# Turned results read two or three units later, and the last quarter of a merged sum turned on TensorE

## The chip, the cores and the metric

The kernel runs on one core of a Trainium2 chip. The metric is the device time of one execution in microseconds (us); the median of several runs is compared.

## The reference

Two decoder layers over 256 tokens of 2048 features, all in float32. Every layer normalises its input, projects it once to some 18,000 columns, and runs three token mixers on slices of that projection; each mixer's output is gated, projected to 2048 columns, weighted with a sigmoid gate and summed; a last projection is added to the input.

```
h = rms_norm(x, norm_w)
proj = h @ w_in
(qa, ka, va, za, qi, ki, wi, ub, zb, qc, kc, vc, zc, gates) = jnp.split(proj, split_points(), axis=-1)
qa = apply_rope(qa...); ka = apply_rope(ka...); qi = apply_rope(qi...); ki = apply_rope(ki...)
y_a = (dsa_attention(qa, ka, va, qi, ki, wi, top_k) * jax.nn.silu(za)) @ w_a_out
y_b = (conformer_conv(ub, conv_w, conv_b, cln_w, cln_b) * jax.nn.silu(zb)) @ w_b_out
y_c = (stick_breaking_attention(qc, kc, vc) * jax.nn.silu(zc)) @ w_c_out
g = jax.nn.sigmoid(gates).reshape(b, s, N_BRANCH, D_MODEL)
merged = g[:, :, 0] * y_a + g[:, :, 1] * y_b + g[:, :, 2] * y_c
return x + merged @ w_out
```

After the second layer comes a final RMSNorm. Branch A picks 64 keys per query with an indexer (qi, ki, wi); branch B is a causal depthwise convolution with 31 taps; branch C is stick-breaking attention.

## The kernel before, in words

**Weights.** Each projection is worked in *units*: 128x1024 weights are loaded into `raw` (four buffers, issued on SyncE), cast on ScalarE to the high part `wh` (`high`, L219), and VectorE takes the difference as the low part `wl` (`low`, L223), three buffers each. A unit's twelve matmuls (L233, in `token_products` or `chunk_T`) give the three products high x high, low x high and high x low. Eight units make a *chunk* of 512 columns. There are 733 units; TensorE runs them one after the other, and VectorE and ScalarE prepare the parts up to three units ahead.

**Turned results.** `chunk_N` leaves tokens on the partitions; most users want features there. `turned` (L255) does that off TensorE: two 32x32-block transposes on VectorE into `zt` (L266), four strided DMAs from GpSimd's queue into `z` in DRAM (L269), one fetch into `zy` (L271; `zt` and `zy` have one buffer each). What is done with `zy` is a generator, the *use*: rope for the queries of attention A (`rope_F`, L365), scaling or copying for C (L785, L834), the SiLU gate (`gate`, L402), a sigmoid and the product into `yT` for the convolution's input (L671, L674), the split of the merged sum (`use_m`, L938) and of the next layer's input (`x_parts_F`, L442).

**When a use runs.** `turned` first finishes any older use (`settle`), issues all five DMAs at once, and puts the use on the list `pending`, due `LATER` = 6 units on (10 for the convolution's input, 5 for the last quarter of the merged sum). After each unit, `background` takes the first use that is due, places its next step behind that unit's last matmul, and the step is scheduled with high priority. All queues are in order: an instruction that waits holds up everything behind it on its engine, weight parts too. A scheduler fixes the order at build time. A step ends at a `yield n`, and the next is due n units on.

**Other work behind the units.** `stages` holds generators for the attention, the indexer (`index_first`, `index`, with `choose`: eight rounds of MAX8 and MATCH_REPLACE8 on VectorE) and the convolution's norm; `waiting` holds the convolution's taps (L417, L419), of which one or two go behind each low part.

**The merged sum.** For each of four quarters `mg` holds the sum; the last branch in the order is B. When its quarter is added (L974, L975), `turned` and `use_m` make its parts `mx`. The output projection `w_out` begins right after the fourth quarter; its units need quarters 0 to 3 in turn, the seventh unit the first rows of quarter 3.

The functions that the diff touches and what calls them, with the line numbers of the profile:

Of the kernel before, what the change touches and what calls it, by code (L numbers as in the profile page):

```python
# [14 lines left out]
P = 128  # L15
# [9 lines left out]
TOPK = 64  # L25
TAPS = 31
PRE = 2
LATER = 6
EV, EV2 = (3,), (5,)
URGENT = 10 ** 6  # L30
PAD = TAPS - 1
# [18 lines left out]
def trunk(ctx: ExitStack, tc: tile.TileContext, x, w_in, xt, w_a, w_b, w_c, w_out,  # L50
# [38 lines left out]
    def nm(s):  # L89
        uid[0] += 1  # L90
        return f"{s}_{uid[0]}"
# [17 lines left out]
    def hi(b, k, n=1, ts=slice(0, S)):  # L109
        return part(b, 0, k, n, ts)  # L110

    def lo(b, k, n=1, ts=slice(0, S)):
        return part(b, 1, k, n, ts)
# [29 lines left out]
    pending = []  # L143

    def step_on(e):
        with tc.high_priority():
            try:
                e[0] = count[0] + next(e[1])
            except StopIteration:
                pending.remove(e)  # L150

    def settle():
        while pending:
            step_on(pending[0])

    def background(mm):
        for e in pending[:1]:
            if e[0] <= count[0]:
                with tc.issue_after(mm.ins):
                    step_on(e)  # L160
        for e in stages[:2]:
            if e[1] <= count[0]:
                with tc.issue_after(mm.ins):
                    advance(e)
                break
# [24 lines left out]
                f()  # L190

    newest = [None]

    def load_unit(w, k0, kn, segs, dst=None):
        n = sum(c for _, c in segs)
# [20 lines left out]

    def high(u):
        with tc.high_priority():
            nc.scalar.copy(u[1], u[0])  # L219

    def low(u):
        with tc.high_priority():
            sub = nc.vector.tensor_sub(u[2], u[0], u[1].bitcast(F32))  # L223
        drain(sub)

    def unit(*args, **kw):
# [27 lines left out]

    def turned(srcs, use, later=LATER):  # L255

        settle()
        n = len(srcs)  # L260
        tmp = tp.tile([P, n, 4, 4, 32], F32, tag="zt", bufs=1, name=nm("zt"))
        z = dp.tile([n, 4, 32, 4, P], F32, tag="z", bufs=4, name=nm("z"))
        y = tp.tile([P, n * 4, 4, 32], F32, tag="zy", bufs=1, name=nm("zy"))
        with tc.high_priority():
            for t, src in enumerate(srcs):
                nc.vector.transpose(tmp[:, t].rearrange("p b k i -> p k b i"),  # L266
                                    src.rearrange("p (k b c) -> p k b c", b=4, c=32))
            for a in range(4):
                nc.gpsimd.dma_start(z[:, :, :, a, :].rearrange("t b c e -> c (t b) e"),  # L269
                                    tmp[a * 32:(a + 1) * 32].rearrange("c t b k i -> c (t b) (k i)"))  # L270
            nc.gpsimd.dma_start(y.rearrange("p (t a) k i -> p t (a k i)", t=n),  # L271
                                z.rearrange("t b c a e -> (b c) t (a e)"))

        pending.append([count[0] + later, use(y)])

    def by_feature(y):
        return y.rearrange("p u k i -> p k u i")

    def blocks(v):
        return v.rearrange("p k (u i) -> p k u i", i=32)  # L280

    def chunk_F(w, c0, act, nk, use, later=LATER):
        turned(chunk_N(w, [(c0, 512)], act, nk), use, later)
# [74 lines left out]
    def split(h, l, src):  # L358
        nc.scalar.copy(h, src)  # L359
        nc.vector.tensor_sub(l, src, h.bitcast(F32))  # L360
# [4 lines left out]
    def rope_F(dst, y):  # L365
        s = t4().rearrange("p (u k i) -> p u k i", k=4, i=32)
        nc.scalar.copy(s[0:64], y[64:128])
        nc.scalar.copy(s[64:128], y[0:64])
        c, d = (v.rearrange("p (u i) -> p u i", i=32).unsqueeze(2).to_broadcast([P, S // 32, 4, 32])
                for v in (cos1, sin1))  # L370
        nc.vector.tensor_mul(y, y, c)
        yield 1
        nc.vector.tensor_mul(s, s, d)
        nc.vector.tensor_add(blocks(dst), by_feature(y), by_feature(s))

# [21 lines left out]
    def sigmoid_of(y):  # L397
        sg = t4().rearrange("p (u k i) -> p u k i", k=4, i=32)
        nc.scalar.activation(sg, y, AF.Sigmoid)  # L399
        return sg  # L400

    def gate(c0, o, b, w, hx):  # L402
        def use(k, y):
            sg = sigmoid_of(y)
            nc.vector.tensor_mul(y, y, sg)  # L405
            yield 1
            nc.vector.tensor_mul(y, y, blocks(o[:, k:k + 4, :]).rearrange("p k u i -> p u k i"))
            split(blocks(hi(b, k, 4)), blocks(lo(b, k, 4)), by_feature(y))

        for k in range(0, KC, 4):  # L410
            chunk_F(w, c0 + k * P, hx, KD, partial(use, k))

    def tap(yT, cv, pr, c, q):
        wq = pr[:, P_CW + c * TAPS + q:P_CW + c * TAPS + q + 1]
# [27 lines left out]
    def x_parts_F(xn, k, nw, y):  # L442
        xT, ux = xn
        xs = xT[k // KC][:, k % KC:k % KC + 4, :]
        nc.vector.tensor_mul(blocks(xs), by_feature(y), nw[:, k:k + 4].unsqueeze(2).unsqueeze(3).to_broadcast([P, 4, S // 32, 32]))
        split_at(ux, k, 4, xs)
        yield 1

    def ssq_total(ssq):
        s = small(2)[:, :ssq.shape[1]]  # L450
# [16 lines left out]
    for layer in range(DEPTH):  # L467
# [200 lines left out]

        def use_g(y):
            sg_u.append(sigmoid_of(y))  # L670
            yield 1  # L671

        def use_a(y, yT=yT):
            nc.vector.tensor_mul(blocks(yT[:, 4:8, PAD:]), by_feature(y), by_feature(sg_u.pop()))  # L674
            taps(1)
            yield 1

        sg_u = []
        with tc.high_priority():
# [1 line left out]
                nc.vector.tensor_mul(yT[:, i * 2:i * 2 + 2, PAD:], ua[i], sgs[i].rearrange("p (h t) -> p h t", h=2))  # L681
        taps(0)
        chunk_F(w, O_UG + 4 * P, hx, KD, use_g)
        chunk_F(w, O_UA + 4 * P, hx, KD, use_a, 10)


        qi = [slot(F32R).rearrange("p a b -> p (a b)").rearrange("p (h t) -> p h t", t=P) for _ in range(2)]
# [90 lines left out]

        qaT = slot()
        for h in range(0, NH, 4):  # L780
            chunk_F(w, O_QA + h * P, hx, KD, partial(rope_F, qaT[:, h:h + 4, :]))
        qcT = slot()

        def use_q(h, y, qcT=qcT):
            nc.scalar.mul(blocks(qcT[:, h:h + 4, :]), by_feature(y), SCALE)  # L785
            yield 1

        for h in range(0, NH, 4):
            chunk_F(w, O_QC + h * P, hx, KD, partial(use_q, h))
# [42 lines left out]

        def use_k(h, y, kcT=kcT):
            nc.scalar.copy(blocks(kcT[:, h:h + 4, :]), by_feature(y))  # L834
            yield 1

        for h in range(0, NH, 4):
            chunk_F(w, O_KC + h * P, hx, KD, partial(use_k, h))
# [98 lines left out]

        def use_m(j, y):  # L938
            split(blocks(hi(mx, j * 4, 4)), blocks(lo(mx, j * 4, 4)), by_feature(y))
            yield 1  # L940

        for b in (0, 2, 1):
            if b == 2:
                finish()
                settle()
                gc = parts(KC)
                gate(O_ZC, qcT, gc, w, hx)
            if b == 1:
                finish()
                settle()  # L950
                gb = parts(KC)
                gate(O_ZB, cv, gb, w, hx)
                mx = parts(KD)
            gx = ga if b == 0 else gc if b == 2 else gb
            for j in range(4):
                if b == 2 and j == 1:
                    finish()
                    flush()
                    start(conv_norm())
                g = chunk_N(w, [(O_G + b * D + j * 512, 512)], hx, KD)  # L960
                sg = [ev() for _ in range(NT)]
                with tc.high_priority():
                    for t in range(NT):
                        nc.scalar.activation(sg[t], g[t], AF.Sigmoid)  # L964
                if j == 0:
                    settle()
                y = chunk_N((w_a, w_b, w_c)[b][layer], [(j * 512, 512)], gx, KC)
                with tc.high_priority():
                    for t in range(NT):
                        dst = mg[j // 2][:, j % 2, t, :]  # L970
                        if b == 0:
                            nc.vector.tensor_mul(dst, y[t], sg[t])
                        else:
                            nc.vector.tensor_mul(sg[t], y[t], sg[t])  # L974
                            nc.vector.tensor_add(dst, dst, sg[t])  # L975
                if b == 1:
                    turned([mg[j // 2][:, j % 2, t, :] for t in range(NT)], partial(use_m, j), LATER if j < 3 else 5)


        last = layer == DEPTH - 1  # L980
# [21 lines left out]
        def emit_x(xc, accs, q, c0, ts):  # L1002
            n = xc.shape[-1]
            with tc.high_priority(offset=URGENT):
                for a_, t in zip(accs, ts):
                    nc.vector.tensor_add(xc[:, t, :], a_, xc[:, t, :])  # L1006
            if last:
                sq = ev()
                for t in ts:
                    with tc.high_priority(offset=URGENT):  # L1010
                        nc.scalar.activation(sq[:, :n], xc[:, t, :], AF.Square, accum_out=ssq[:, t, q:q + 1])
                    nc.vector.tensor_mul(xfr[t][:, c0:c0 + n], xc[:, t, :], fwr[:, c0:c0 + n])
            else:
                x_squares([xc[:, t, :] for t in ts], ssq, q, ts)
                if q < 3:
                    turned([xc[:, t, :] for t in ts], partial(x_parts_F, xn, c0 // P, nwn))

        def store_x(xc, c0):
            if not last:
# [98 lines left out]
```

## Time and profile before

| | us |
|---|---|
| median of 3 runs | 2071.09 |
| lowest, highest | 2069.34, 2073.09 |
| the profiled execution | 2067.06 |
| its span | 2065.1 |
| TensorE busy | 2039.8 |
| VectorE busy | 1498.5 |
| ScalarE busy | 1036.4 |

The span runs from the first to the last recorded instruction; 1.96 us lie around it. Busy time counts an engine's instructions, not its waiting; of TensorE's matmuls the ends are modelled, so that their starts are the better measure. In the profile PE is TensorE, PEld its weight load, DVE is VectorE, ACT is ScalarE, POOL is GpSimd, SP is SyncE, and L233 is line 233 of the kernel.

### The profile page before, as it was taken

Reading aid. Unit: us, or ns where it says so; the run is one execution under the profiler, and the core shown is the slowest. Engines: PE = TensorE matmul, PEld = TensorE weight load, DVE = VectorE, ACT = ScalarE, POOL = GpSimd, SP = SyncE. Lnnn points to the kernel's source line nnn. Section 1 sums busy time; section 2 is a strip of 40 time slices with the busy share of each in tenths; the row PEclk is TensorE's granted clock in tenths of the full one; section 3 lists DMA queues with packets and bytes.
Section 4 is the critical chain, followed back from the end, with each engine's and each line's share of the span. In section 5 each row is a group of like instructions: output and inputs, shape, how many; then the busy total and the mean of one; then the engine's idle time right before and its main releaser. Section 6 shows DMA issues by size and latency. Waiting matters only on the chain.

```text
span 2065.1 us, 26913 instructions
## 1 busy us (share of the span) xinstructions
PE 2039.8 (99%) x10064; PEld 1739.5 (84%) x10064; DVE 1498.5 (73%) x2026; ACT 1036.4 (50%) x1217; POOL 119.2 (6%) x199
## 2 busy tenths in 40 slices
PE   9999999999999999999999999999999999999998
PEld 9899878888888888888898998788888888888877
DVE  8768988688777855665676799886887678556555
ACT  7455445466444544444454654454664445444443
POOL 0100011010000001011101001110100000011000
PEclk9999999999999999999999999999999999999999
DMA  7777576665567567876767775766755665677764
GB/s 255 229 224 215 163 225 214 200 221 168 174 197 230 190 198 227 262 233 227 252 198 232 215 207 169 229 213 194 223 165 176 208 219 192 193 234 248 251 210 147
DMA packets 246531, 435.08 MB, mean 211 GB/s; under 512 B 19712, under 2 KB 69888, under 8 KB 246272
## 3 DMA queue, kind: packets, MB, share of 16 engines
q1 hardware_dynamic: 231632, 389.32, 59.3%
q0 software_dynamic: 13104, 40.91, 6.5%
q10 hardware_dynamic: 1664, 3.15, 0.4%
q8 instruction: 78, 1.28, 0.3%
q14 instruction: 53, 0.43, 0.1%
HBM read 408.67 MB, written 24.64 MB: 210 GB/s over the span
## 4 chain that ended last, share of the span: by engine, by line
PE 46%; DMA 2%; DVE 2%; issue 1%; ACT 0%; POOL 0%; DVEq 0%; POOLq 0%; ACTq 0%
PE acc L233 44%; DMA zy<-z 1%; DMA z<-zt 1%; DVE wl L223 1%; PE mm L764 0%; PE mm L797 0%; POOL z L269 0%; PE mm L822 0%; DVE zt L266 0%; PE mm L891 0%; PE mm L855 0%; DVE s L419 0%; DVE t L1006 0%; PE mm L814 0%; ACT wh L219 0%
## 5 line engine op out<-in xcount | busy, mean ns | idle before, releaser
L233 PE MATMUL acc<-wh,s 128*128 128x512 f32 (+2 forms) x4992 | 1222.4, 387 | 7.8 <-ACT wh L219 5.2
L223 DVE TENSOR_TENSOR wl<-raw,wh 128x1024 fp32r<-128x1024 f32 (+2 forms) x729 | 876.9, 1207 | 409.3 <-ACT wh L219 407.5
L219 ACT CAST wh<-raw 128x1024 fp32r<-128x1024 f32 (+2 forms) x728 | 756.3, 1043 | 796.8 <-PE acc L233 559.9
L233 PEld LDWEIGHTS acc<-wh,s 128*128 128x128 f32 x4992 | 923.5, 188 | 196.1 <-ACT wh L219 7.7
L233 PE MATMUL acc<-wl,s 128*128 128x512 f32 (+2 forms) x2496 | 658.1, 386 | 1.2 <-DVE wl L223 1.2
L233 PEld LDWEIGHTS acc<-wl,s 128*128 128x128 f32 x2496 | 464.2, 188 | 96.5 <-DVE wl L223 2.1
L419 DVE SCALAR_TENSOR_TENSOR s<-yT,cst,s 128x256 f32<-128x256 f32 x480 | 216.3, 478 | 0.4
L233 PE MATMUL acc<-s,wh 128*128 128x256 f32 (+2 forms) x1120 | 194.2, 320 | 0.0
L269 POOL DMA_DIRECT2D z<-zt x156 | 91.0, 590 | 1667.5 <-DVE zt L266 1520.2
L233 PEld LDWEIGHTS acc<-s,wh 128*128 128x128 f32 x1120 | 169.2, 191 | 3.4
L233 PE MATMUL acc<-s,wl 128*128 128x192 f32 (+1 forms) x864 | 115.9, 276 | 5.6 <-DVE wl L223 5.6
L233 PEld LDWEIGHTS acc<-s,wl 128*128 128x128 f32 x864 | 111.7, 191 | 8.5 <-DVE wl L223 7.6
L266 DVE STREAM_TRANSPOSE zt<-acc 128x512 f32<-128x512 f32 x56 | 39.8, 710 | 11.4 <-PE acc L233 11.4
L271 POOL DMA_DIRECT2D zy<-z x39 | 28.0, 719 | 193.7 <-DMA z<-zt 151.2
L359 ACT CAST s<-zy 128x1024 fp32r<-128x1024 f32 x20 | 21.0, 1050 | 32.1 <-DMA zy<-z 18.1
L360 DVE TENSOR_TENSOR s<-zy,s 128x1024 fp32r<-128x1024 f32 x20 | 24.5, 1223 | 16.7 <-ACT s L359 16.7
L974 DVE TENSOR_TENSOR ev<-acc,ev 128x512 f32<-128x512 f32 x32 | 22.0, 688 | 19.2 <-PE acc L233 19.2
L405 DVE TENSOR_TENSOR zy<-zy,t 128x1024 f32<-128x1024 f32 x12 | 14.7, 1224 | 18.9 <-ACT t L399 18.8
L399 ACT ACTIVATE t<-zy 128x1024 f32<-128x1024 f32 x14 | 14.9, 1061 | 26.5 <-DMA zy<-z 26.4
L964 ACT ACTIVATE ev<-acc 128x512 f32<-128x512 f32 x48 | 26.3, 591 | 0.0
L384 DVE TENSOR_TENSOR ev<-ev,cst 128x384 f32<-128x384 f32 (+2 forms) x20 | 11.2, 558 | 19.4 <-ACT ev L382 19.3
L975 DVE TENSOR_TENSOR s<-s,ev 128x512 f32<-128x512 f32 x32 | 21.9, 684 | 0.0
(203 smaller groups left out, 813.3 us busy)
## 6 DMA issues: line engine op xcount, KB each, us to landing
raw<-in_w_in_dram SPq DMA_DIRECT2D x555, 512.0 KB, 3.6
raw<-in_w_out_dram SPq DMA_DIRECT2D x64, 512.0 KB, 4.9
z<-zt POOLq DMA_DIRECT2D x156, 128.0 KB, 4.4
zy<-z POOLq DMA_DIRECT2D x39, 512.0 KB, 5.0
raw<-in_w_a_dram SPq DMA_DIRECT2D x32, 512.0 KB, 3.5
raw<-in_w_c_dram SPq DMA_DIRECT2D x32, 512.0 KB, 3.6
raw<-in_w_b_dram SPq DMA_DIRECT2D x32, 512.0 KB, 5.0
raw<-in_w_in_dram SPq DMA_DIRECT2D x16, 256.0 KB, 2.8
```

Of the source, the lines that this page charges most:

```text
L219: nc.scalar.copy(u[1], u[0])
L223: sub = nc.vector.tensor_sub(u[2], u[0], u[1].bitcast(F32))
L233: newest[0] = nc.tensor.matmul(o, lhsT, rhs, start=start, stop=stop, skip_group_check=True)
L266: nc.vector.transpose(tmp[:, t].rearrange("p b k i -> p k b i"), src.rearrange("p (k b c) -> p k b c", b=4, c=32))
L269: nc.gpsimd.dma_start(z[:, :, :, a, :].rearrange("t b c e -> c (t b) e"), tmp[a * 32:(a + 1) * 32].rearrange("c t b k i -> c (t b) (k i)"))
L271: nc.gpsimd.dma_start(y.rearrange("p (t a) k i -> p t (a k i)", t=n), z.rearrange("t b c a e -> (b c) t (a e)"))
L359: nc.scalar.copy(h, src)
L360: nc.vector.tensor_sub(l, src, h.bitcast(F32))
L419: nc.vector.scalar_tensor_tensor(o, yT[:, c, q:q + S], wq, o, op0=ALU.mult, op1=ALU.add)
L964: nc.scalar.activation(sg[t], g[t], AF.Sigmoid)
L974: nc.vector.tensor_mul(sg[t], y[t], sg[t])
L975: nc.vector.tensor_add(dst, dst, sg[t])
```

## The change

- A use, or the next step of one, is placed behind the newest unit's two parts (the copy of `high` and the difference of `low`) in the order, and no longer behind the newest unit's last matmul. All uses that are due go, not one per unit.
- `LATER` becomes 9. Gates, rope and the next layer's input use 8, the convolution's input 11. The single steps after a use (`yield 1` at its end) become `yield 0`, and in `rope_F` and `gate` the `yield 1` moves one operation up.
- `turned` no longer calls `settle`. The buffer `zy` is taken, and its fetch issued, in a first step two units after the transposes; the use is due later by the rest.
- The fourth quarter of the merged sum is no longer turned through DRAM: a stage `turn` transposes it in eight 128x128 pieces on TensorE, behind the second unit of the output projection, into PSUM, and splits it from there.

```diff
-LATER = 6
+LATER = 9
...
     def step_on(e):
-        with tc.high_priority():
+
+        with tc.high_priority(), tc.issue_after(newest_parts[0].ins), tc.issue_after(newest_parts[1].ins):
...
     def background(mm):
-        for e in pending[:1]:
-            if e[0] <= count[0]:
-                with tc.issue_after(mm.ins):
-                    step_on(e)
+        while pending and pending[0][0] <= count[0]:
+            step_on(pending[0])
...
-            nc.scalar.copy(u[1], u[0])
+            newest_parts[0] = nc.scalar.copy(u[1], u[0])
...
-            sub = nc.vector.tensor_sub(u[2], u[0], u[1].bitcast(F32))
+            newest_parts[1] = sub = nc.vector.tensor_sub(u[2], u[0], u[1].bitcast(F32))
...
-        settle()
         n = len(srcs)
...
-        y = tp.tile([P, n * 4, 4, 32], F32, tag="zy", bufs=1, name=nm("zy"))
...
+        def rest():
+            y = tp.tile([P, n * 4, 4, 32], F32, tag="zy", bufs=1, name=nm("zy"))
             nc.gpsimd.dma_start(y.rearrange("p (t a) k i -> p t (a k i)", t=n),
                                 z.rearrange("t b c a e -> (b c) t (a e)"))
-
-        pending.append([count[0] + later, use(y)])
+            yield later - 2
+            yield from use(y)
+
+        pending.append([count[0] + 2, rest()])
...
         nc.scalar.copy(s[64:128], y[0:64])
+        yield 1
...
         nc.vector.tensor_mul(y, y, c)
-        yield 1
         nc.vector.tensor_mul(s, s, d)
...
             sg = sigmoid_of(y)
+            yield 1
             nc.vector.tensor_mul(y, y, sg)
-            yield 1
...
-            chunk_F(w, c0 + k * P, hx, KD, partial(use, k))
+            chunk_F(w, c0 + k * P, hx, KD, partial(use, k), LATER - 1)
...
-        chunk_F(w, O_UA + 4 * P, hx, KD, use_a, 10)
+        chunk_F(w, O_UA + 4 * P, hx, KD, use_a, LATER + 2)
...
-            chunk_F(w, O_QA + h * P, hx, KD, partial(rope_F, qaT[:, h:h + 4, :]))
+            chunk_F(w, O_QA + h * P, hx, KD, partial(rope_F, qaT[:, h:h + 4, :]), LATER - 1)
...
+        def turn(j, mg=mg):
             yield 1
+            ps = mm_tile().rearrange("p (k t) -> p k t", t=S)
+            for kk in range(4):
+                for t in range(NT):
+                    nc.tensor.transpose(ps[:, kk, t * P:(t + 1) * P], mg[j // 2][:, j % 2, t, kk * P:(kk + 1) * P],
+                                        ident)
+            with tc.high_priority():
+                split_at(mx, j * 4, 4, ps)
...
-                if b == 1:
-                    turned([mg[j // 2][:, j % 2, t, :] for t in range(NT)], partial(use_m, j), LATER if j < 3 else 5)
+                if b == 1 and j < 3:
+                    turned([mg[j // 2][:, j % 2, t, :] for t in range(NT)], partial(use_m, j))
+                elif b == 1:
+                    start(turn(j))
...
-                    turned([xc[:, t, :] for t in ts], partial(x_parts_F, xn, c0 // P, nwn))
+                    turned([xc[:, t, :] for t in ts], partial(x_parts_F, xn, c0 // P, nwn), LATER - 1)
```

In the changed kernel's own line numbers the transposes of `turn` are L950.

More of the change, by code (lines that the diff above doesn't have):

```diff
@@ L192, in trunk @@
     newest = [None]
+    newest_parts = [None, None]
     def load_unit(w, k0, kn, segs, dst=None):
@@ L446, in x_parts_F @@
         split_at(ux, k, 4, xs)
-        yield 1
+        yield 0
     def ssq_total(ssq):
@@ L670, in use_g @@
             sg_u.append(sigmoid_of(y))
-            yield 1
+            yield 0
         def use_a(y, yT=yT):
@@ L675, in use_a @@
             taps(1)
-            yield 1
+            yield 0
         sg_u = []
@@ L785, in use_q @@
             nc.scalar.mul(blocks(qcT[:, h:h + 4, :]), by_feature(y), SCALE)
-            yield 1
+            yield 0
         for h in range(0, NH, 4):
@@ L834, in use_k @@
             nc.scalar.copy(blocks(kcT[:, h:h + 4, :]), by_feature(y))
-            yield 1
+            yield 0
         for h in range(0, NH, 4):
@@ L939, in use_m @@
             split(blocks(hi(mx, j * 4, 4)), blocks(lo(mx, j * 4, 4)), by_feature(y))
+            yield 0
+        def turn(j, mg=mg):
             yield 1
+            ps = mm_tile().rearrange("p (k t) -> p k t", t=S)
[5 more added lines that the diff above has]
+                split_at(mx, j * 4, 4, ps)
         for b in (0, 2, 1):
```

## The prediction

> **What bounds the kernel now.** I read the page's head first, then the waits of TensorE, then its timeline round each wait, then the engine that released it.
>
> ```profile
> span 2065.1 us, 26913 instructions
> PE 2039.8 (99%) x10064; PEld 1739.5 (84%) x10064; DVE 1498.5 (73%) x2026; ACT 1036.4 (50%) x1217; POOL 119.2 (6%) x199
> ```
>
> ```profile
> PE acc L233 <- DVE wl L223: 6.9, 6, 1.7
> PE acc L233 <- ACT wh L219: 5.2, 4, 2.8
> PE acc L233 <- ACT s L359: 2.6, 2, 2.3
> ```
>
> TensorE is busy 99% of the span, so nothing can be gained but its pauses, and the matmuls stay as they are. The second fence (engine and line, releaser, us in all, times, longest) names them: it waits for a weight's low part (DVE), a weight's high part (ACT), or the merged sum's parts. They lie at three kinds of place, each once in both layers. I price a place by the starts of successive weight units in TensorE's timeline (start, duration; a unit begins with its row "wh").
>
> Place A, the first query-index chunks after the convolution's input:
>
> ```profile
> 110.90 1.59 PE L233 MATMUL acc<-s,wh 128*128 128x384 f32 x8
> ...
> 121.45 1.57 PE L233 MATMUL acc<-s,wh 128*128 128x384 f32 x8
> ```
>
> ```profile
> 1135.40 1.59 PE L233 MATMUL acc<-s,wh 128*128 128x384 f32 x8
> ...
> 1145.87 1.58 PE L233 MATMUL acc<-s,wh 128*128 128x384 f32 x8
> ...
> 1148.15 1.59 PE L233 MATMUL acc<-s,wh 128*128 128x384 f32 x8
> ```
>
> An undisturbed unit takes 2.28 us (1145.87 to 1148.15). Between the other two rows of the second layer lie three units: 10.47 us, so 10.47 - 6.84 = 3.63 us are lost. In the first layer it is 10.55 - 6.84 = 3.71. Place A costs 7.34 us.
>
> Place B, the second half of attention A's queries, where rope's use of the turned result runs:
>
> ```profile
> 274.25 1.98 PE L233 MATMUL acc<-wh,s 128*128 128x512 f32 x8
> ...
> 279.09 2.76 PE L233 MATMUL acc<-wh,s 128*128 128x512 f32 x8 [1.97 <-ACT wh L219]
> ...
> 283.36 2.18 PE L233 MATMUL acc<-wh,s 128*128 128x512 f32 x8
> ```
>
> ```profile
> 1279.62 1.99 PE L233 MATMUL acc<-wh,s 128*128 128x512 f32 x8
> ...
> 1282.35 1.98 PE L233 MATMUL acc<-wh,s 128*128 128x512 f32 x8
> ...
> 1298.67 1.98 PE L233 MATMUL acc<-wh,s 128*128 128x512 f32 x8
> ...
> 1304.36 3.66 PE L233 MATMUL acc<-wh,s 128*128 128x512 f32 x8 [2.81 <-ACT wh L219]
> ...
> 1308.78 2.00 PE L233 MATMUL acc<-wh,s 128*128 128x512 f32 x8
> ```
>
> A unit takes 2.72 us here (1279.62 to 1282.35 is 2.73). In the second layer two units took 1308.78 - 1298.67 = 10.11, so 4.67 are lost: 2.97 of waiting and 1.70 because the unit after it ran slowly (4.42 for 2.72). In the first layer 9.11 - 5.44 = 3.67, of which the slow unit is 4.27 - 2.72 = 1.55. Place B costs 8.34 us.
>
> Place G, the start of the output projection, which needs the last quarter of the merged sum:
>
> ```profile
> 954.79 1.98 PE L233 MATMUL acc<-wh,s 128*128 128x512 f32 x8
> ...
> 964.40 1.98 PE L233 MATMUL acc<-wh,s 128*128 128x512 f32 x8
> ```
>
> ```profile
> 1978.96 1.98 PE L233 MATMUL acc<-wh,s 128*128 128x512 f32 x8
> ...
> 1987.42 2.46 PE L233 MATMUL acc<-wh,s 128*128 128x512 f32 x9 [2.33 <-ACT s L359]
> ...
> 1990.63 1.98 PE L233 MATMUL acc<-wh,s 128*128 128x512 f32 x8
> ```
>
> In both stretches lie 37 matmuls (three units and one matmul pulled ahead), 37/12 x 2.72 = 8.39 us. The first lasts 9.61, the second 11.67: 1.22 + 3.28 = 4.50 us lost.
>
> **The change, part by part.** I compared the order in which the two programs' instructions stand on each engine; a "place" below is the number of weight units whose part stands ahead in that queue. TensorE's order is the same but for place G. Of the uses on ScalarE, those of the gates and of the merged sum stand where they stood (the first gate's split alone is one later); nine reads per layer stand one to three later. So the change moves little, and A, B and G must be walked.
>
> *Place A.* The product into yT (L674) moves on VectorE from behind unit 405's low part to behind unit 410's.
>
> ```profile
> 1136.18 1.23 DVE L674 TENSOR_TENSOR yT<-zy,t 128x1024 f32<-128x1024 f32 x1 [6.02 <-DMA zy<-z]
> ```
>
> Before, L674 sat 6.02 us at the head of the in-order queue until zy landed, and the next low parts behind it: that is the whole of A. Its turn had come at 1136.18 - 6.02 = 1130.16; five units of 2.28 us later it comes at about 1141.6, 5.4 us after the landing. The fetch into zy is now issued two units after the turn, but it waits anyway for the last part of z, so the landing stays. The 1.23 us of L674 now falls between rope's steps of another chunk; with three buffers for each part, VectorE may run that late there without TensorE noticing. A goes: -7.34. If the cover is gone (a landing 5 us later) A stays.
>
> *Place B.* ScalarE's first read of the second chunk (L367) stands behind unit 468's high part in both programs; only L368 goes behind the next one.
>
> ```profile
> 1301.14 1.04 ACT L367 COPY t<-zy 64x1024 f32<-64x1024 f32 x1 [6.47 <-DMA zy<-z]
> ...
> 1303.26 2.94 ACT L219 CAST wh<-raw 128x1024 fp32r<-128x1024 f32 x3
> ```
>
> So the 6.47 us of waiting for zy stay, and the cast that TensorE waits for, once behind both reads (3.26 - 1.14 = 2.12 us for the two), comes one read, 1.06 us, sooner. Against that the chunk's transposes (and with them z and zy) come later: ahead of them on VectorE, which has no idle time there (the third busy time of the row below, 12.00 of 12.00 us), the change puts one more MATCH_REPLACE8 and one more MAX8 of `choose` and one first tap less.
>
> ```profile
> 1278.00:1290.00 12.00, 11.41 (x50) 9.47 (x51) 12.00 (x22) 4.42 (x5) 2.34 (x4) 1.00 0.64 195
> ```
>
> ```profile
> 1274.67 0.09 DVE L723 MATCH_VALUE_LOAD sc<-sm,sc 128x8 f32 x1
> 1274.74 0.41 DVE L723 MATCH_REPLACE8 sc<-sm,sc 128x256 f32<-128x256 f32 x1
> 1275.46 0.42 DVE L722 MAX8 sm<-sc 128x8 f32<-128x256 f32 x1
> ...
> 1284.06 0.39 DVE L417 TENSOR_SCALAR s<-yT,cst 128x256 f32<-128x256 f32 x1
> ```
>
> 0.09 + 0.41 + 0.42 - 0.39 = 0.53 later. Net 0.53 sooner per layer. Whether the slow unit goes too is read from the clock:
>
> ```profile
> 279.00:283.40 4.40, 4.31 (x13) 3.40 (x14) 4.40 (x5) 2.98 (x4) 0.00 (x0) 0.65 0.39 128
> 1304.00:1308.80 4.80, 4.44 (x13) 3.56 (x14) 4.80 (x5) 2.95 (x4) 0.00 (x0) 0.64 0.36 111
> 1987.00:1992.00 5.00, 4.58 (x20) 3.60 (x21) 3.37 (x3) 2.37 (x3) 0.00 (x0) 1.00 0.23 69
> ```
>
> The third figure from the right is the granted clock. Pauses of 1.97 and 2.81 us brought it to 0.65 and 0.64, one of 2.33 us did not, and none of at most 1.7 us (the longest at A) did. The first layer's pause shrinks to about 1.4 us: its slow unit goes, 1.55. The second's shrinks to about 2.3 us: I let it stay. B: -(2 x 0.53 + 1.55) = -2.6, with bounds under the rivals.
>
> The Trainium skill (TensorE: Matmul & The Clock Gate, Part 1) has the array fall to half clock only after an idle window of about 3.4 us. The trace disagrees, having the fall at 1.97 us; by the page neither slow unit would be there after, and the sum below would be 1.7 us lower.
>
> *Place G.* Four strided DMAs, a fetch and two VectorE transposes go; eight transposes on TensorE and a split out of PSUM come. The same eight, with the same 128x128 shape:
>
> ```profile
> 1377.26 2.09 PE L233 MATMUL acc<-wh,s 128*128 128x512 f32 x8
> ...
> 1380.91 2.07 PE L233 MATMUL acc<-wh,s 128*128 128x512 f32 x8
> ```
>
> Between these starts lie one unit and eight transposes (L814): 3.65 - 2.72 = 0.93 us. Two layers: +1.86. The transposes stand behind the projection's second unit, about when VectorE writes the sum's last piece; should they wait for it, such an addition is the price:
>
> ```profile
> L975 DVE TENSOR_TENSOR s<-s,ev 128x512 f32<-128x512 f32 x32 | 21.9, 684 | 0.0
> ```
>
> so 0.7 us a layer at most. The split's copy stands behind the fifth unit's high part, its difference behind the sixth's low part, and the seventh needs them: both lie beside the matmuls of units three to six. G: -4.50 + 1.86 = -2.64.
>
> The Trainium skill (the same page, Part 4) says that transposes do not count as busy for the clock, which speaks against this edit. The trace shows the granted clock at full speed past L814, and the unit behind it at 2.7 us; by the rule the price is the rival below.
>
> *Sum.* -7.34 - 2.6 - 2.64 = -12.6 us. The profiled execution took 2067.06 us (span 2065.1): it would take 2054.5. That execution was 4.0 us under the median of the runs, 2071.09; I take the same off there: 2058.5.
>
> **The rivals.**
>
> *Landing earlier (chance 0.10).* L367's wait hangs on two transfers that share the DMA engines with weight loads. The fetch took 4.2 us at A and 6.6 at B, from these issues to the ends of the waits of L674 and L367:
>
> ```profile
> 1131.98 0.72 POOL L271 DMA_DIRECT2D zy<-z  x1 [4.14 <-ACT ev L288]
> ...
> 1294.54 0.72 POOL L271 DMA_DIRECT2D zy<-z  x1 [5.09 <-DMA z<-zt]
> ```
>
> 2.4 us sooner at B with 0.53 gained would leave almost no pause. Then B loses its waits, both slow units included: at most -8.3 instead of -2.6, so -18.3 and 2052.8.
>
> *Landing later, or VectorE's denser `choose` holding low parts up (0.20).* By the same 2.4 us the other way, less 0.53, B loses 1.9 us a layer and keeps its slow units: -7.34 - 2.64 + 3.8 = -6.2, 2064.9. For it: VectorE's full row above.
>
> *Time given back (0.10).* TensorE, earlier by A, catches up with VectorE in the same stretch and waits there. Against: VectorE's own 6.02 us of idling go too. Price: A's 7.34, so -5.3, 2066; spread round that, half of it lies within what can be told from no change.
>
> *The transposes slow the clock (0.05).* Two slow units of about 1.6 us: -9.4, 2061.7.
>
> *Slower (0.10).* zy is one buffer. Uses that stand up to three units later release it later, so the next fetch, the next landing and ScalarE's next wait come later. From the point where the release passes the landing of z, each of the four pushed uses (queries and keys of attention C) would cost a layer what B costs, 4.67: 8 x 4.67 - 12.6 = +25, 2096. Against: two to three units are 5 to 8 us, and the next chunk takes eight units.
>
> *The change doesn't do what it says:* most uses don't move, which is in the forecast.
>
> **How the numbers follow.** The forecast has 0.45, with its own range of 2056 to 2061. The range 2051 to 2067 takes in both landings and most of the time given back. About 0.2% (4.1 us) is what a measurement of this kernel can tell from no change: slower 0.10; same 0.07, half of the time given back and the end of the late landings; faster 0.83.
>
> **What would show it.** Right: no wait of TensorE for wl among the query-index chunks, L674 without idle time before it; L367 of the second chunk still waiting 5 us or more for zy, and TensorE behind it for the cast; no "s L359" among TensorE's waits, and eight L950 transposes in 0.8 to 0.9 us. Wrong: a wait for wl or wh at a new place, an idle stretch before L950, or no pause at B.

## The result, and the profile after

The changed kernel takes 2051.28 us (median of 4, 2050.54 to 2052.27); the kernel before took 2070.22 (4 runs, 2065.00 to 2073.09). The ratio is 0.9912, interval 0.9891 to 0.9932. Timed twice more, in other sets, it was 0.9928 (0.9912 to 0.9945) and 0.9930 (0.9918 to 0.9942). So it is faster by 0.7 to 0.9%. The forecast was 2058.5, with a range of 2051 to 2067: the time lies 0.3 us inside its low end, and outside the 2056 to 2061 that the forecast itself was given. The profiled execution took 2050.71 us, 16.35 less than that of before, where 12.6 less was forecast.

The page's head and TensorE's waits (engine and line, releaser, us in all, times, longest) of the changed kernel:

```profile
span 2048.9 us, 26913 instructions
PE 2036.2 (99%) x10080; PEld 1738.4 (85%) x10080; DVE 1496.9 (73%) x2022; ACT 1036.1 (51%) x1217; POOL 113.1 (6%) x189
```

```profile
PE acc L233 <- ACT wh L219: 2.8, 3, 1.1
PE mm L604 <- DVE eps L72: 1.1, 1, 1.1
PE acc L233 <- DVE wl L223: 0.6, 2, 0.3
PE mm L436 <- DVE t L1021: 0.3, 1, 0.3
```

Waiting for low parts fell from 6.9 to 0.6 us, for high parts from 5.2 to 2.8, and the wait for the merged sum's parts is gone.

*Place A.* VectorE's timeline:

```profile
1130.44 2.35 DVE L223 TENSOR_TENSOR wl<-raw,wh 128x1024 fp32r<-128x1024 f32 x2
1133.82 1.23 DVE L223 TENSOR_TENSOR wl<-raw,wh 128x1024 fp32r<-128x1024 f32 x1 [1.02 <-ACT wh L219]
1134.96 1.22 DVE L677 TENSOR_TENSOR yT<-zy,t 128x1024 f32<-128x1024 f32 x1
```

The product into yT (L677 now) starts right behind a low part: there is no bracket on its row, where before it showed 6.02 us of idling for the DMA.

*Place B.* ScalarE and TensorE in the second layer:

```profile
1289.51 1.05 ACT L370 COPY t<-zy 64x1024 f32<-64x1024 f32 x1 [4.74 <-DMA zy<-z]
1290.59 1.04 ACT L219 CAST wh<-raw 128x1024 fp32r<-128x1024 f32 x1
1291.65 1.05 ACT L371 COPY t<-zy 64x1024 f32<-64x1024 f32 x1
1292.73 2.96 ACT L219 CAST wh<-raw 128x1024 fp32r<-128x1024 f32 x3
```

```profile
1287.69 1.98 PE L233 MATMUL acc<-wh,s 128*128 128x512 f32 x8
...
1291.68 2.11 PE L233 MATMUL acc<-wh,s 128*128 128x512 f32 x8 [1.11 <-ACT wh L219]
...
1294.53 1.98 PE L233 MATMUL acc<-wh,s 128*128 128x512 f32 x8
```

ScalarE's first read still waits 4.74 us for zy, but one cast stands between the two reads. TensorE waits 1.11 us where it waited 2.81. The two units take 1294.53 - 1287.69 = 6.84 us, 1.40 over 5.44, where 4.67 were lost, and the second of them takes 2.85 us, not 4.42. Not all of this is the cast's: the fetch into zy that this read waits for was issued at 1284.55 us and was read 4.96 us later, where the kernel before needed 6.60.

```profile
1284.55 0.72 POOL L272 DMA_DIRECT2D zy<-z  x1 [5.58 <-DMA z<-zt]
```

*Place G.* TensorE at the start of the second layer's output projection:

```profile
1957.03 1.03 PE L950 MATMUL mm<-cst,s 128*128 128x128 f32 x8
1957.82 2.07 PE L233 MATMUL acc<-wh,s 128*128 128x512 f32 x8
1959.73 1.07 PE L233 MATMUL acc<-wl,s 128*128 128x512 f32 x4
1960.64 1.98 PE L233 MATMUL acc<-wh,s 128*128 128x512 f32 x8
```

Eight transposes wait for nothing, and the units follow without a bracket.

Where the time went is seen best from the starts of the same matmul in both traces; a stretch lost or won time by as much as the difference changes over it:

| stretch (starts in the trace of before) | before minus after, from | to | won | forecast |
|---|---|---|---|---|
| A, first layer (110.90 to 121.45) | 0.01 | 3.68 | 3.67 | 3.71 |
| B, first layer (274.24 to 283.36) | 3.65 | 6.28 | 2.63 | 2.08 |
| G, first layer (940.06 to 964.40) | 6.76 | 7.09 | 0.33 | 0.29 |
| A, second layer (1135.40 to 1145.87) | 7.65 | 11.24 | 3.59 | 3.63 |
| B, second layer (1298.67 to 1308.78) | 10.98 | 14.25 | 3.27 | 0.53 |
| G, second layer (1959.92 to 1990.63) | 13.77 | 16.16 | 2.39 | 2.35 |
| all else | | | 0.28 | 0 |
| sum | | | 16.16 | 12.6 |

A and G came out within 0.1 us of the forecast; B won 5.90 us instead of 2.6.

### The profile page after: what moved, and what is told of

It is laid out like the page before. It is cut to its first block, busy times and chain, and to the rows that moved or that the text cites. A ratio compares the mean times of both kernels' runs of the same rounds, so it can differ in the third digit from the quotient of the medians.

```text
span 2048.9 us, 26913 instructions
## 1 busy us (share of the span) xinstructions
PE 2036.2 (99%) x10080; PEld 1738.4 (85%) x10080; DVE 1496.9 (73%) x2022; ACT 1036.1 (51%) x1217; POOL 113.1 (6%) x189
## 4 chain that ended last, share of the span: by engine, by line
PE 47%; DVE 2%; issue 1%; DMA 0%; ACT 0%; DVEq 0%; POOLq 0%
PE acc L233 46%; DVE wl L223 1%; DVE s L422 0%; DVE sc L773 0%; PE mm L800 0%; DMA zy<-z 0%; DVE sc L726 0%; PE mm L825 0%; PE mm L894 0%; PE mm L858 0%; DVE sm L725 0%; ACT wh L219 0%; PE mm L817 0%; PE mm L880 0%; PE mm L861 0%
## 5 line engine op out<-in xcount | busy, mean ns | idle before, releaser
L267 POOL DMA_DIRECT2D z<-zt x148 | 86.3, 590 | 1629.0 <-DVE zt L264 1482.8
```

## The experiments

Two theories stood against each other. Mine: three separate places, A from the product's new place on VectorE, B from one cast that passes a read, G from the transposes. The rivals: the longer delays carry it all, or the fetches land earlier whatever the order. "Units" are places in a queue, as in the prediction. Times are against the kernel before in the same set (2068.75, 2068.66 and 2066.68 us by median in the three sets), or against the changed kernel in the same set.

**place_only: the placement alone.**

```diff
     def step_on(e):
-        with tc.high_priority():
+        with tc.high_priority(), tc.issue_after(newest_parts[0].ins), tc.issue_after(newest_parts[1].ins):
...
-                with tc.issue_after(mm.ins):
-                    step_on(e)
+                step_on(e)
```

> The kernel before with one edit: a step of a use is placed behind the newest unit's two parts; all delays, the settling and the last quarter stay. On every engine the order is that of before, but for the product into yT (L674 of before), which goes from 405 to 409 units (39 to 43). Theory: this product is all of place A. It comes 4 x 2.28 = 9.1 us later and its 6.0 us of waiting go: about -7.2 us against before, no wait of TensorE for low parts among the query-index chunks, places B and G as before (8.3 and 4.5 us lost). Rival (the longer delays carry the gain, the place does little): no change. Rival (the time is given back to VectorE, which is full later): -5 or less lost, that is -2 us.

2059.80 us, ratio 0.9955 (0.9940 to 0.9970): 9 us faster than before, with an interval of 6 to 12. VectorE's row of the product in this kernel has no wait:

```profile
1138.25 1.22 DVE L674 TENSOR_TENSOR yT<-zy,t 128x1024 f32<-128x1024 f32 x1
```

So this edit, which moves one instruction a layer, is all of A and about half of the whole gain. TensorE's trace shows something more. B still has pauses (1.70 and 1.95 us by the starts of matmuls), but no slow unit behind them, and a new pause stands in the next chunk, at the first read of attention C's queries (ScalarE, then TensorE):

```profile
1318.85 1.06 ACT L785 ACTIVATE s<-zy 128x1024 f32<-128x1024 f32 x1 [6.49 <-DMA zy<-z]
```

```profile
1320.90 2.12 PE L233 MATMUL acc<-wh,s 128*128 128x512 f32 x8 [1.18 <-ACT wh L219]
```

In the profile of before ScalarE waits there as well, and TensorE does not; in that of the changed kernel the read stands one unit later, waits less, and TensorE does not pause either (before, then after):

```profile
1325.31 1.06 ACT L785 ACTIVATE s<-zy 128x1024 f32<-128x1024 f32 x1 [5.28 <-DMA zy<-z]
```

```profile
1313.63 1.06 ACT L788 ACTIVATE s<-zy 128x1024 f32<-128x1024 f32 x1 [4.14 <-DMA zy<-z]
```

**late_only: the delays without the placement.**

```diff
     def step_on(e):
-        with tc.high_priority(), tc.issue_after(newest_parts[0].ins), tc.issue_after(newest_parts[1].ins):
+        with tc.high_priority():
...
-            step_on(pending[0])
+            with tc.issue_after(mm.ins):
+                step_on(pending[0])
```

> The changed kernel with the placement undone: a step of a use goes behind the newest unit's last matmul again; the longer delays, the missing settling, the late fetch and the transposes of the last quarter stay. Theory: with high priority, the delay alone moves nothing on ScalarE and VectorE (the product into yT stands at 39 and 405 units as before, the reads of rope at 93, 93, 102, 102), so A and B stay and only place G goes: -2.3 us against before. Rival (the delay is what helps): -15 or more.

2063.91 us, ratio 0.9973 (0.9962 to 0.9984): 4.8 us. The product into yT waits as before (its line is L678 here):

```profile
1136.15 1.23 DVE L678 TENSOR_TENSOR yT<-zy,t 128x1024 f32<-128x1024 f32 x1 [6.17 <-DMA zy<-z]
```

The delays alone do nothing to A: a step tied to a matmul is late in the program, but with high priority it is put into its own engine's queue as early as before. Tied to an instruction of that engine, it moves.

**no_delay: placement and transposes, the delays of before.**

```diff
-LATER = 9
+LATER = 6
...
-        chunk_F(w, O_UA + 4 * P, hx, KD, use_a, LATER + 2)
+        chunk_F(w, O_UA + 4 * P, hx, KD, use_a, 10)
```

The three uses at `LATER - 1` were set to `LATER`, so that every delay is that of before.

> The changed kernel with the delays of before (6, and 10 for the convolution's input). The product into yT stands at 43 and 409 units, the reads of rope at 102 and 468 units, both ahead of the next cast, as before. Theory: A and G go, B stays with its pauses of 2 to 3 us and its slow units: -7.2 - 2.3 = -9.5 us against before. Rival (the placement alone is enough at B too): -16 to -19.

2056.65 us, ratio 0.9939 (0.9921 to 0.9958): 12.1 us, between the two theories, and the sum of place_only's 9.0 and g_only's 4.9 within their intervals. Its profile shows pauses of 1.70 and 1.68 us at B and 1.25 and 1.28 at C's first read. What is missing to the changed kernel is thus the delays' part, 3 to 4 us, and by this profile it lies at B and C.

**g_only: the transposes alone**, in the kernel before:

```diff
-                if b == 1:
-                    turned([mg[j // 2][:, j % 2, t, :] for t in range(NT)], partial(use_m, j), LATER if j < 3 else 5)
+                if b == 1 and j < 3:
+                    turned([mg[j // 2][:, j % 2, t, :] for t in range(NT)], partial(use_m, j))
+                elif b == 1:
+                    start(turn(j))
```

> The kernel before with the last quarter of the merged sum turned on TensorE in eight transposes behind the second unit of the output projection, nothing else. Theory: 4.5 us of waiting go, 1.9 us of transposes come: -2.3 us as the two traces have it (-2.6 as predicted), eight transposes in 0.9 us a layer, no wait for the sum's parts. Rival (the waits are only moved): no change. Rival (the transposes slow the clock): +0.6.

2063.82 us, ratio 0.9975 (0.9964 to 0.9987): 4.9 us, with an interval of 2.7 to 7.4. **no_g** is the other way about, the changed kernel with the last quarter turned through DRAM:

> The changed kernel, but the last quarter of the merged sum is turned through DRAM again, due 5 units on. Theory: place G adds up with the rest, so +2.3 us against the changed kernel, with the wait for the sum's parts back at the start of the output projection (1 to 3 us a layer). Rival (without the other pauses G is covered): no change or -1.9, since eight transposes a layer go.

2058.30 us against 2053.00 of the changed kernel in its set: +5.3. So the edit saves time, and the clock is not slowed. Its size is nearer 5 us by these medians than the 2.7 that the two traces show, though the intervals take in 2.7. In no_g's profile G itself lost only 0.4 us a layer, less than the 0.8 us of the eight transposes, so there the rival's account (G is covered) fits. By the starts of the same matmuls, about 6.5 us were lost at the end of the first layer instead:

```profile
PE acc L233 <- ACT wh L219: 4.2, 6, 1.2
PE acc L233 <- DVE wl L223: 2.9, 3, 2.3
PE mm L436 <- DVE t L1019: 1.7, 1, 1.7
```

The wait of 2.3 us for a low part and that of 1.7 us are there (TensorE at 1026 to 1031 us), behind VectorE's 5.73 us for the last fetch into zy, and a granted clock of 0.50 from 1028.2 to 1035.1 us makes up the rest; in the changed kernel this wait of VectorE took 2.97. Whether the four DMAs of the last quarter, which no_g issues again, caused that, or chance, one profile can't tell. So the medians show that the edit saves time, and what it saves beyond G's own 2.7 us stays open.

**after_again**, the changed kernel beside the next three, and **after_third**, beside the last three:

> The changed kernel itself, for comparison with the others of this set: 2051.3 us, as measured, with runs within 2 us of each other.

> The changed kernel itself, for comparison within this set: 2051 to 2053 us.

2053.00 and 2051.63 us. The forecast of runs within 2 us of each other failed in the first of the two: one of its six runs took 2058.07.

**reads_together: the cast between rope's two reads.**

```diff
-            chunk_F(w, O_QA + h * P, hx, KD, partial(rope_F, qaT[:, h:h + 4, :]), LATER - 1)
+            chunk_F(w, O_QA + h * P, hx, KD, partial(rope_F, qaT[:, h:h + 4, :]), LATER - 3)
```

> The changed kernel with rope's use of attention A due 6 units on instead of 8. In the second chunk both of ScalarE's reads then stand ahead of the next cast again (102, 102 and 468, 468 units; in the changed kernel 102, 103 and 468, 469); all the rest is as in the changed kernel. Theory: what saves time at B is one cast that passes the second read, and through it the clock: each pause grows by one read, 1.06 us, to about 2.0 and 2.3 us, and a slow unit of 1.5 us comes behind it in each layer: +2.1 to +5.2 us against the changed kernel. Rival (the transfers land earlier in the changed kernel, whatever the order of the reads): less than +1.

2056.98 us against 2053.00: +4.0, inside the theory's bounds. ScalarE:

```profile
1291.31 1.05 ACT L370 COPY t<-zy 64x1024 f32<-64x1024 f32 x1 [5.83 <-DMA zy<-z]
1292.37 1.04 ACT L371 COPY t<-zy 64x1024 f32<-64x1024 f32 x1
1293.44 2.95 ACT L219 CAST wh<-raw 128x1024 fp32r<-128x1024 f32 x3
```

The reads stand together, and TensorE's pauses grow to 1.83 and 1.89 us. No slow unit came, and against after_again's profile the pauses at B are 1.9 us longer, of the 4.0 us; two other pauses (2.13 and 1.70 us, at the last gate of the convolution's branch) are of a kind that the changed kernel has in some executions too. The edit is not confined to the one cast: on VectorE `choose`, the taps and the chunk's transposes trade places again as well, so the run undoes the whole of the change at B.

**rope_later: the reads two to three units later**, the same line with `LATER + 1`:

> The changed kernel with rope's use of attention A due 10 units on instead of 8: both reads of the second chunk stand at 105 and 471 units, two to three units later than now. Theory: their wait for the landing (4.7 us in the first layer) is covered by two to three units of 2.72 us, and what is left of place B, pauses of 0.9 and 1.3 us, goes: -2.2 us against the changed kernel. Rival (the later products of rope run into the part of the stretch where VectorE is full, and low parts come late): +1 to +3.

2049.75 us against 2053.00: -3.25. In its profile both pauses at B are gone, though that execution was one of its longest (2053.86), with a pause of 2.95 us and a slow unit at the last gate of the convolution's branch. Timed again:

> The kernel of the earlier run with rope's use due 10 units on, timed again beside the changed kernel. Theory: -2 to -3 us against it, for want of the two pauses at B; its profiled execution of the first run had a chance pause of 2.95 us at the last gate of the convolution's branch, not a cost of the edit. Rival (that pause belongs to the edit): no change.

2050.38 us against 2051.63: -1.25, less than forecast. The pause of 2.95 us is not in this profile (one of 1.69 us stands at the same gate in the second layer), so it came by chance. B in ScalarE's row, with almost no wait left:

```profile
1289.18 1.05 ACT L370 COPY t<-zy 64x1024 f32<-64x1024 f32 x1 [0.21 <-DMA zy<-z]
```

This version beats both kernels, the changed one by little: median of its 11 runs 2050.31 (2047.9 to 2053.9), of the changed kernel's 15 runs 2051.85 (2050.5 to 2058.1).

**c_reads_earlier: attention C's query reads one unit earlier.**

```diff
-            chunk_F(w, O_QC + h * P, hx, KD, partial(use_q, h))
+            chunk_F(w, O_QC + h * P, hx, KD, partial(use_q, h), LATER - 1)
```

> The changed kernel with the first use of attention C's queries due 8 units on instead of 9, so that ScalarE's reads stand at 110 and 118 units (476 and 484) instead of 111 and 119 (477 and 485). Theory: the changed kernel also saves a pause that the first profile of before hid behind its slow units: in the kernels whose first C read stands at 110, TensorE lost 1.3 to 1.8 us there in all four profiles where no slow unit came before. So pauses of about 1 us a layer come back in that chunk, +1 to +3 us. Rival (that pause comes from late weights, whatever the place of the read): no change.

2059.28 us against 2051.63: +7.65, more than the theory's 1 to 3. ScalarE and TensorE:

```profile
1319.55 1.06 ACT L788 ACTIVATE s<-zy 128x1024 f32<-128x1024 f32 x1 [7.06 <-DMA zy<-z]
```

```profile
1321.60 3.63 PE L233 MATMUL acc<-wh,s 128*128 128x512 f32 x8 [2.65 <-ACT wh L219]
```

Pauses of 1.95 and 2.81 us came back at C, each at the first of a layer's two reads, the second with a slow unit (1.73): 6.5 us in an execution that was the longest of its six (2062.73). In the profiles of place_only, no_delay and g_only, whose reads stand at the same places, the two pauses at C made 2.5 to 3.1 us, without a slow unit. What makes up the rest of the 7.65 us in the executions that were not profiled is not shown.

**no_residual_load: the changed kernel without the residual's loads.**

```diff
-            if layer == 0:
-                nc.sync.dma_start(xc, xin[:, :, c0:c0 + n])
-            else:
-                nc.sync.dma_start(xc, x1[:, :, c0:c0 + n].rearrange("t p d -> p t d"))
+            nc.gpsimd.memset(xc, 0.0)
```

> The changed kernel without the loads of the residual for the output projection (the four buffers are zeroed on GpSimd instead, so the input is not added to the layer's result). Theory: the pauses of 1 to 3 us at the last gate of the convolution's branch, which come in some executions only, are the fetch into zy sharing the DMA engines with three of these loads of 512 KB issued 1 to 4 us behind it. Without them the fetch lands in about 4.5 us instead of 6.6, no pause is left there, the runs lie closer together, and the median falls by 1 to 3 us. Rival (the fetch is slow for other reasons): pauses there as before, no change.

2051.34 us against 2051.63: no change, so the forecast for the median failed. The profile agrees with the mechanism as far as one execution can: no pause is left at the two gates, and in the second layer ScalarE reads zy 5.42 us after the fetch's issue (1834.97 to 1840.39; about 4.5 was forecast), where it took 7.14 in the changed kernel's third profile (1835.35 to 1842.49) and 5.97 and 6.22 in the two others. But a pause of 1.2 us stands at the end of the first layer. The residual's loads cost no more than the runs' spread.

## Why the prediction was right or wrong, point by point

- *The number.* It fell inside the range with some luck. A and G, 9.98 of the 12.6 us, came by the forecast's mechanism and size; two other steps, B and the one from the execution to the median, were off, both to the same side, and the low end of the range had been set for the rival of an earlier landing.
- *What bounds the kernel.* Right: only TensorE's pauses could be won, and the gain is theirs, stretch by stretch.
- *Place A, -7.34.* Right: -7.26 in the trace. place_only and late_only show that the placement does it and the longer delay does not, which the prediction did not separate.
- *Place G, -2.64.* Right in the traces (-2.72; the transposes wait for nothing); the medians of g_only and no_g say about 5, and the difference is open. The granted clock stayed at full speed behind the transposes:

```profile
1957.00:1962.00 5.00, 5.00 (x28) 4.26 (x26) 3.43 (x3) 2.45 (x3) 0.00 (x0) 1.00 0.64 204
```

  The rule that speaks against the edit (the Trainium skill, TensorE: Matmul & The Clock Gate, Part 4) thus cost nothing at eight transposes.
- *Place B, -2.6.* The mechanism was right, the size wrong: -5.90. The step at fault took the two pauses of one profile as a constant. With both reads ahead of the cast, twelve pauses (two in each of the profiles of before, place_only, late_only, g_only, no_delay and reads_together) went from 1.22 to 2.97 us, mean 1.85; with the cast between them, twelve (the changed kernel's three profiles, no_g, c_reads_earlier and no_residual_load) from 0.80 to 1.60, mean 1.20. The net gain of the pause is 0.65 us, close to the 0.53 forecast. But the second layer's pause before was the longest of its kind (2.97, of which I let 2.3 stay, with a slow unit). Three of the first twelve had a slow unit behind them, none of the later twelve, of which none was over 1.60 us. So part of the 5.90 is the draw of this pair of profiles: the waits of ScalarE's first read in it fell by 0.71 and 1.73 us. What the change takes from B in most executions is nearer 1.3 us for two layers, and a slow unit of 1.6 us where one came.
- *Uses standing one to three units later, costed at nothing.* Wrong at C: c_reads_earlier shows that one unit at C's reads saves 7.65 us by its medians, of which pauses at C, as other profiles show them, are 2.5 to 3.1 us for two layers. The profile of before did not show that loss. Where a slow unit stands at B (both layers of before, the first of late_only), TensorE does not pause at C; where none stands and the read is at 110 or 476 units, it pauses by 1.25 to 2.81 us, 9 times of 9. So the slow unit's 1.6 us appear to have been cover for C (no run removed the slow unit alone), and taking them away alone gives them back there. B's 1.3 us and C's 2.5 to 3.1 together are about the 3 to 4 us that no_delay lacked. The rival "time given back" was right as a mechanism, at another place than it was put, and the change's own delay of C's reads prevents it.
- *The landing rivals.* The time resembles "landing earlier" (2052.8), and in this pair of profiles the landing at B's second layer did come 1.64 us sooner after its issue (4.96 for 6.60 us); the wait left, 4.72 and 4.74 us, is a little under the 5 that the prediction named as its sign. But the change did not cause it: with both reads ahead of the cast, the first read waited 4.85 to 6.47 us in the twelve cases, mean 5.31; with the cast between them 4.72 to 6.06, mean 5.37. The 6.47 of before was the outlier.
- *The step from the execution to the median.* Wrong: the 4.0 us between the profiled execution of before (2067.06) and its median (2071.09, 3 runs) were carried over. In the later sets the median of before was 2068.75 (29 runs), 2068.66 and 2066.68 (11 each): three runs of a kernel that varies from 2063 to 2075 are no offset. The changed kernel's execution lay 0.57 us under its own median. This step makes 3.4 of the 7.2 us between forecast and result; B makes 3.3.
- *Slower through the single zy.* Did not come: no landing was late enough to stall a new place.

## What to carry to other kernels

When a queue is in order, ask of each instruction that waits for a transfer what stands behind it, and move that one; to move it in the schedule, tie it to an instruction of its own engine's queue, since a later due time tied to another engine's instruction left ScalarE's reads at B and C, and the product at A, where they were. A pause in one profile is one draw: before it is priced, look at the same place in the other layer and in other runs, and ask what a stall was covering, because the next wait in line (here C's read) appears when the first is gone. Carry a gain from trace to trace, and the spread of the runs beside it, not one execution's distance from a median of three.

## What the runs showed of the hardware that was not expected

Whether the clock falls behind a pause is not a matter of its length alone. Measured by the starts of matmuls, of 77 pauses of 0.6 to 2.0 us in the fourteen profiles one was followed by slow units, and all three of 2.81 to 2.97 us were. Of nine between 2.06 and 2.49, three were (2.06, 2.13 and 2.45 us) and five were not; the ninth (no_g, 2.44 us) had the one of the 77, 1.88 us, close behind it, and the clock fell during that second one. Two rows of all engines, with the granted clock third from the right: behind a pause of 2.06 us at B (late_only) it fell, behind one of 2.13 us at a gate (reads_together) it did not:

```profile
279.50:283.50 4.00, 3.94 (x12) 3.14 (x13) 4.00 (x5) 2.95 (x4) 0.00 (x0) 0.68 0.38 99
```

```profile
827.60:831.60 4.00, 3.95 (x17) 3.25 (x18) 4.00 (x5) 2.32 (x3) 0.00 (x0) 1.00 0.36 105
```

What tells them apart is where the pause lies. In all fourteen profiles the granted clock changes only at points a whole number of 3.413 us apart, and it stays at 0.50 for 3.41 us (five times) or 6.83 us (twice). Cut the spans at these points, without their first 10 and last 20 us: eight stretches at full clock hold 2.06 us or more of pauses (every pause over 0.15 us is counted). The six with 2.13 to 2.94 us are followed by half clock, and of the two with 2.06 us one is. None of the 86 with 0.6 to 1.89 us is. The pause of 2.13 us in the first row below (before, at B) lies whole in one such stretch, the row behind it is the half clock; the 2.13 us of reads_together is split, with 1.49 us in the longer part.

```profile
276.92:280.33 3.41, 1.44 (x6) 1.05 (x6) 2.33 (x3) 3.38 (x4) 0.00 (x0) 1.00 0.47 145
280.33:283.74 3.41, 3.41 (x9) 2.64 (x8) 3.41 (x5) 1.65 (x2) 0.00 (x0) 0.50 0.52 158
```

The Trainium skill (TensorE: Matmul & The Clock Gate, Part 1) names an idle window of about 3.4 us; here about 2.1 us of pauses inside such a stretch were enough, so the measurement decides.

The same fetch into zy, that of the last gate in the second layer, was read 5.97, 6.22 and 7.14 us after its issue in three profiles of the changed kernel. Where a read stands close behind a landing, such differences are pauses: the runs of before lie between 2063.1 and 2075.4 us, fourteen of the changed kernel's fifteen between 2050.5 and 2053.9. That the landings make the whole of the spread was not shown.
